# A gated mixer and peer-expert block: 160 of 512 tokens by gathered expert rows instead of 128, the dense units in groups of eight

## The chip, the cores and the metric

The program runs on one core of one Trainium2 chip. The metric is the device time of one execution in microseconds, the median of several. Engines are named as the profile names them: PE is TensorE (PEld its weight loads), DVE is VectorE, ACT is ScalarE, POOL is GpSimd, which issues the indirect DMAs, and SP is the engine whose queue issues the plain ones.

## What is computed

One layer of a model with 512 tokens of width 2048 (a retention branch and an mLSTM branch, merged and projected), then a residual block of "peer" experts and a final norm. The change touches the peer block alone:

```python
def block(tb):                       # tb: 128 tokens x 2048
    qh = (tb @ w_query).reshape(128, 8, 2, 128)
    s = jnp.einsum('thpd,hpkd->thpk', qh, sub_keys)
    sv, si = lax.top_k(s, 16)
    cand_s = sv[:, :, 0, :, None] + sv[:, :, 1, None, :]     # 16 x 16 sums
    cand_i = si[:, :, 0, :, None] * 128 + si[:, :, 1, None, :]
    best_s, best_j = lax.top_k(cand_s.reshape(128, 8, 256), 16)
    eid = jnp.take_along_axis(cand_i.reshape(128, 8, 256), best_j, axis=-1)
    g = jax.nn.softmax(best_s, axis=-1)
    act = gelu(jnp.einsum('thkd,td->thk', expert_down[eid], tb))
    return jnp.einsum('thk,thkd->td', g * act, expert_up[eid])
```

So each token picks 8 heads x 16 = 128 of 16,384 experts; an expert is a row of 2048 in `expert_down` and one in `expert_up`.

## The kernel before

Channels lie on partitions and tokens along the free axis. A float32 matrix product is made of three float32r matmuls: a weight tile `raw` (128 x 1024 from HBM) is split into `ws`, a high half cast on ScalarE and a low half subtracted on VectorE (`weight`), the activations likewise, and `mm3` adds high x high, high x low and low x high. There are seven `raw` and three `ws` buffers. A scheduler lets weight tiles run up to 400 steps ahead of their place in the program.

The peer block (`phase_d`) has three stages. `select` computes the queries (16 tiles of w_query, each 16 blocks of 128 channels by `mm3` on all 512 tokens), scores and picks the experts, mostly on VectorE. `gating` turns the picks of the dense tokens into a table of gates in HBM, by one-hot products. `experts` then evaluates the two kinds of tokens:

- The dense tokens go through all experts as through a wide hidden layer: 128 tiles of 128 hidden units each. A tile's down part is 48 matmuls (`hidden`, PSUM tile `hid`), then gelu on ScalarE (`hf`), the product with the gates (`hf` again, VectorE) and the split into `hh` (ScalarE and VectorE). After a group of GRP tiles their up part runs: 16 output blocks, of which four stay in PSUM all the while (`pac`) and twelve are added to `acc` in SBUF after each group (`upp`). 38 tiles' down parts (NE) run earlier, beside `select` and `gating`, and are parked in HBM.
- The first 128 tokens are *gathered*: one token on each partition, and for each of its 128 picks an indirect DMA on GpSimd brings one row of 2048 for every partition (`row`, 1 MB). For the down table VectorE multiplies it with the tokens (`h2n`) and sums to `dots`; for the up table it adds the row times its weight to `gacc`.

The order of the gathers is written out by hand. `gather(n)` counts units of TensorE's work: 20 for a hidden tile (in two halves) and UP for each of the eight steps of a group's up part (UP0 while the group's tiles were all computed earlier), and calls `row()` whenever the share of rows issued falls behind the share of SPAN. Each call issues a gather and lets VectorE process the one before (LAG = 1). A gather waits for its buffer, one of two (ROW_BUFS), and by `add_manual_dep` for the matmul last issued at its place (`self.last`).

```python
if len(late) > LAG or not slots:
    f, s_, r = late.pop(0)
    f(s_, r)
```

## Time and profile before

| | before |
|---|---|
| median of 3 runs | 4233.39 us |
| lowest, highest | 4217.9, 4237.24 us |
| the profiled execution's own time | 4242.06 us |
| its span, first to last instruction | 4240.3 us |
| PE busy | 4113.0 us (97%) |
| PEld busy | 3668.2 us (87%) |
| DVE busy | 2829.7 us (67%) |
| ACT busy | 1333.7 us (31%) |
| mean granted PE clock (share of full speed) | 0.988 |
| HBM read, written | 851.24, 63.05 MB |

Busy time is the time in which an engine had an instruction in it. Matmuls are pipelined: one starts before the last has ended, so what one costs is read from start to start and not from its length. DVE here means VectorE's own instructions, waits not included. The name before an arrow is the tile that is written, those behind it are read.

### The profile page before, as it was taken

To read this page: it belongs to the slowest core of one execution; us is meant where nothing else is said; L and a number is where in the kernel's file an instruction comes from. 1 tells how busy PE (TensorE), PEld (TensorE's weight loads), DVE (VectorE), ACT (ScalarE), POOL (GpSimd) and SP (SyncE) were. 2 spreads that over 40 slices of the span, in tenths; PEclk is the share of its full clock that TensorE was granted. 3 is DMA by queue.
4 is the path that set the end of the run, shared out by engine and by line. 5 is a ranking of instruction groups with operands and counts; after the bars stand their busy time and mean duration, and the time that the engine had idled before them with its cause. 6 is when DMAs were issued, how large, how long until landed. Compare 5 with 4: busy or idle time off the path is not lost.

```text
span 4240.3 us, 55153 instructions
## 1 busy us (share of the span) xinstructions
PE 4113.0 (97%) x21737; PEld 3668.2 (87%) x21737; DVE 2829.7 (67%) x4504; ACT 1333.7 (31%) x1793; POOL 336.6 (8%) x264
## 2 busy tenths in 40 slices
PE   7999999999999999999999999999999999999998
PEld 3788887777788887898999999999999999999998
DVE  7932238677533433888886766777777777777777
ACT  3322133345322222433443322222323232222223
POOL 0000000000000000000000111111212112111210
PEclk9999999999999999999999999999999999999999
DMA  8522237667633443433456776787878788777784
GB/s 305 203 69 85 70 114 283 218 226 242 223 112 125 150 148 141 147 114 114 166 219 232 257 255 235 287 293 280 297 284 295 285 294 296 285 290 290 293 291 146
DMA packets 288355, 917.90 MB, mean 216 GB/s; under 512 B 26848, under 2 KB 100320, under 8 KB 253664
## 3 DMA queue, kind: packets, MB, share of 16 engines
q1 hardware_dynamic: 248928, 641.74, 43.3%
q0 software_dynamic: 36864, 268.45, 16.7%
q10 hardware_dynamic: 2304, 4.20, 0.3%
q8 instruction: 170, 2.79, 0.3%
q14 instruction: 89, 0.73, 0.1%
HBM read 851.24 MB, written 63.05 MB: 216 GB/s over the span
## 4 chain that ended last, share of the span: by engine, by line
PE 58%; DMA 24%; DVE 9%; issue 8%; ACT 1%; SPq 0%; POOL 0%; DVEq 0%; POOLq 0%; ACTq 0%
DMA row<-in_dnr,eid 11%; PE px L233 9%; PE px L234 9%; PE px L235 9%; DMA row<-in_up,eid 6%; PE hid L233 4%; PE hid L235 4%; PE hid L234 4%; DVE ws L224 3%; DMA gt<-gd 3%; PE va L233 2%; PE va L234 2%; PE va L235 2%; PE upp L235 2%; PE upp L233 2%
## 5 line engine op out<-in xcount | busy, mean ns | idle before, releaser
L223 ACT CAST ws<-raw 128x1024 fp32r<-128x1024 f32 x770 | 809.2, 1051 | 1921.0 <-PE px L235 571.0
L224 DVE TENSOR_TENSOR ws<-raw,ws 128x1024 fp32r<-128x1024 f32 x770 | 939.4, 1221 | 539.2 <-ACT ws L223 534.3
L235 PE MATMUL hid<-h,ws 128*128 128x384 f32 x2048 | 688.1, 336 | 8.7 <-DVE ws L224 8.6
L233 PE MATMUL hid<-h,ws 128*128 128x384 f32 x2048 | 694.9, 339 | 0.2 <-ACT ws L223 0.2
L234 PE MATMUL hid<-h,ws 128*128 128x384 f32 x2048 | 686.2, 335 | 0.0
L233 PE MATMUL upp<-hh,ws 128*128 128x384 f32 x1536 | 520.2, 339 | 19.2 <-DVE acc L1440 16.8
L235 PE MATMUL upp<-hh,ws 128*128 128x384 f32 x1536 | 518.9, 338 | 11.8 <-DVE ws L224 11.8
L234 PE MATMUL upp<-hh,ws 128*128 128x384 f32 x1536 | 517.7, 337 | 0.0
L1263 POOL DMA_INDIRECT row<-in_dnr,eid x128 | 172.0, 1344 | 3071.5 <-DMA gt<-gd 2270.0
L233 PE MATMUL px<-hhi,ws 128*128 128x512 f32 x1024 | 413.1, 403 | 0.0
L1269 DVE SCALAR_TENSOR_TENSOR row<-row,h2n 128x2048 f32<-128x2048 f32 x128 | 293.2, 2291 | 177.0 <-DMA row<-in_dnr,eid 176.9
L234 PE MATMUL px<-hlo,ws 128*128 128x512 f32 x1024 | 407.3, 398 | 0.0
L235 PE MATMUL px<-hhi,ws 128*128 128x512 f32 x1024 | 407.2, 398 | 0.0
L1278 DVE SCALAR_TENSOR_TENSOR gacc<-row,wts,gacc 128x2048 f32<-128x2048 f32 x127 | 298.5, 2350 | 161.0 <-DMA row<-in_up,eid 161.0
L235 PEld LDWEIGHTS hid<-h,ws 128*128 128x128 f32 x2048 | 384.9, 188 | 13.8 <-DVE ws L224 13.4
L233 PEld LDWEIGHTS hid<-h,ws 128*128 128x128 f32 x2048 | 385.3, 188 | 1.1 <-ACT ws L223 0.6
L234 PEld LDWEIGHTS hid<-h,ws 128*128 128x128 f32 x2048 | 385.3, 188 | 0.4
L233 PEld LDWEIGHTS upp<-hh,ws 128*128 128x128 f32 x1536 | 291.3, 190 | 26.9 <-issue 11.3
L235 PEld LDWEIGHTS upp<-hh,ws 128*128 128x128 f32 x1536 | 291.4, 190 | 14.8 <-DVE ws L224 14.7
L234 PEld LDWEIGHTS upp<-hh,ws 128*128 128x128 f32 x1536 | 291.2, 190 | 0.0
L235 PEld LDWEIGHTS px<-hhi,ws 128*128 128x128 f32 x1024 | 192.6, 188 | 47.1 <-issue 2.9
L234 PEld LDWEIGHTS px<-hlo,ws 128*128 128x128 f32 x1024 | 192.7, 188 | 42.2 <-issue 4.6
(426 smaller groups left out, 6198.9 us busy)
## 6 DMA issues: line engine op xcount, KB each, us to landing
raw<-in_dn SPq DMA_DIRECT2D x256, 512.0 KB, 4.1
raw<-in_upt SPq DMA_DIRECT2D x256, 512.0 KB, 4.7
raw<-in_wada_r SPq DMA_DIRECT2D x160, 512.0 KB, 4.6
raw<-in_wt SPq DMA_DIRECT2D x130, 512.0 KB, 3.7
gd<-sg SPq DMA_DIRECT2D x12, 2048.0 KB, 7.5
gt<-gd SPq DMA_DIRECT2D x32, 768.0 KB, 9.5
raw<-in_wada_s SPq DMA_DIRECT2D x32, 512.0 KB, 6.4
raw<-in_wn SPq DMA_DIRECT2D x32, 512.0 KB, 3.6
```

The costliest lines, as they stand in the source:

```text
L223: self.S.copy(w[:, 0], r)
L224: self.V.tensor_sub(w[:, 1], r, w[:, 0].bitcast(F32))
L233: mm(out, lhsT=l[0], rhs=r[0], start=start, stop=False)
L234: mm(out, lhsT=l[0], rhs=r[1], start=False, stop=False)
L235: return mm(out, lhsT=l[1], rhs=r[0], start=False, stop=stop)
L1263: i = G.indirect_dma_start(out=r, out_offset=None, in_=src, in_offset=bass.IndirectOffsetOnAxis(ap=eid[:, s_:s_ + 1], axis=0))
L1269: V.scalar_tensor_tensor(r, r, 1.0, self.h2n, op0=OP.mult, op1=OP.mult, accum_out=dots[:, s_:s_ + 1])
L1278: V.scalar_tensor_tensor(gacc, r, wts[:, s_:s_ + 1], gacc, op0=OP.mult, op1=OP.add)
```

## The change

32 more tokens are gathered. Since there are 128 partitions, each of these tokens stands on four of them (`h2n[1]` holds 32 tokens four times over), and each of the four takes a quarter of the token's 128 picks; so they need 32 gathers in the down table and 32 in the up table, of the same size as the others: 320 in place of 256. The quarters are added at the end by 16 small products with a folded identity (`fold`). Indices and gates of these tokens are brought into that layout by eight small DMAs.

The dense tokens are 352 in place of 384. Because the tokens of a query matmul now lie in two tiles (`h2`, the dense 352, and `h2g`, the gathered 160, which is given back after `select`), each query matmul of 512 columns is written as one of 352 and one of 160. `x1`'s buffers are five in place of eight.

Groups have eight tiles in place of four (GRP), so `acc` is added to half as often; `upt` is laid out in two halves of four tiles a group. UP and UP0 are doubled with it, and SPAN comes to 3644 units for 320 gathers, where it was 3852 for 256.

```diff
-X1_BUFS = 8
+X1_BUFS = 5
-ND = T - P
-GRP = 4
+GX = 32
+G_ = P + GX
+ND = T - G_
+NDB = -(-ND // P)
+GRP = 8
...
-HID, UP, UP0 = 20, 10, 6
+SLOTS = P + GX
+
+
+
+
+HID, UP, UP0 = 20, 10 * GRP // 4, 6 * GRP // 4
...
-        self.h2n = d0.tile([P, D], F32, name="h2n", tag="h2n")
-        self.HF = []
+        self.h2n = [d0.tile([P, D], F32, name=f"h2n{i}", tag=f"h2n{i}") for i in range(2)]
+        self.HG, self.HD = [], []
...
-            h = d0.tile([P, 2, T], F32R, name="h2", bufs=KT)
-            S.activation(h[:, 0], x, AF.Identity, bias=sh2[:, k:k + 1])
-            V.scalar_tensor_tensor(h[:, 1], x, sh2[:, k:k + 1], h[:, 0].bitcast(F32), op0=OP.add, op1=OP.subtract)
-            self.HF.append((h[:, 0], h[:, 1]))
+            h = d0.tile([P, 2, ND], F32R, name="h2", bufs=KT)
+            hg = d1x.tile([P, 2, G_], F32R, name="h2g", bufs=KT)
+            for o, c in ((h, slice(G_, T)), (hg, slice(0, G_))):
+                S.activation(o[:, 0], x[:, c], AF.Identity, bias=sh2[:, k:k + 1])
+                V.scalar_tensor_tensor(o[:, 1], x[:, c], sh2[:, k:k + 1], o[:, 0].bitcast(F32), op0=OP.add, op1=OP.subtract)
+            self.HD.append((h[:, 0], h[:, 1]))
+            self.HG.append((hg[:, 0], hg[:, 1]))
...
+            S.activation(xn[:, k % 4, P:].rearrange("p (q t) -> p q t", t=GX),
+                         x[:, P:G_].unsqueeze(1).to_broadcast([P, P // GX, GX]), AF.Identity, bias=sh2[:, k:k + 1])
...
+            for b, n, o in ((0, P, self.eid[0]), (1, GX, ex)):
+                ef = d1.tile([P, 16], F32, name="ef")
+                V.scalar_tensor_tensor(ef[:n], sel[:n, b, 0, h], float(NKEY), sel[:n, b, 1, h], op0=OP.mult, op1=OP.add)
+                V.tensor_copy(o[:, h], ef[:n])
+            if h == P_H - 1:
+                V.tensor_copy(self.gates[0], sel[:, 0, 2].rearrange("p h k -> p (h k)"))
+                for o, x in ((self.eid[1], ex), (self.gates[1], sel[:GX, 1, 2])):
+                    x = x.rearrange("p h k -> p (h k)")
+                    for q in range(P // GX):
+                        SY.dma_start(o[q * GX:(q + 1) * GX], x[:, q * GX:(q + 1) * GX])
+
+        parts = lambda ps: [(ps[:, G_:], lambda k: self.HD[k]), (ps[:, :G_], lambda k: self.HG[k])]
...
-                    self.tjob([a["wq"][j, 0], a["wq"][j, 1]], [(ps, lambda k: self.HF[k])])
+                    self.tjob([a["wq"][j, 0], a["wq"][j, 1]], parts(ps), one=True)
...
+        def rows(src, i, s_):
             r = d2.tile([P, D], F32, name="row", bufs=ROW_BUFS)
-            i = G.indirect_dma_start(out=r, out_offset=None, in_=src,
-                                     in_offset=bass.IndirectOffsetOnAxis(ap=eid[:, s_:s_ + 1], axis=0))
-            self.tc.add_manual_dep(i.ins, self.last.ins.name, PACE, reason="pace of the gathers")
+            g = G.indirect_dma_start(out=r, out_offset=None, in_=src,
+                                     in_offset=bass.IndirectOffsetOnAxis(ap=eid[i][:, s_:s_ + 1], axis=0))
+            self.tc.add_manual_dep(g.ins, self.last.ins.name, PACE, reason="pace of the gathers")
             return r
...
-        def down(s_, r):
-            V.scalar_tensor_tensor(r, r, 1.0, self.h2n, op0=OP.mult, op1=OP.mult, accum_out=dots[:, s_:s_ + 1])
-            if s_ == P - 1:
-                S.activation(wts, dots, AF.Gelu)
-                V.tensor_mul(wts, wts, gates)
-
-        def up(s_, r):
+        def down(i, s_, r):
+            V.scalar_tensor_tensor(r, r, 1.0, self.h2n[i], op0=OP.mult, op1=OP.mult, accum_out=dots[i][:, s_:s_ + 1])
+            if s_ == dots[i].shape[1] - 1:
+                S.activation(wts[i], dots[i], AF.Gelu)
+                V.tensor_mul(wts[i], wts[i], self.gates[i])
...
-        slots = [(f, w, s_) for f, w in ((down, a["dnr"]), (up, a["up"])) for s_ in range(P)]
+                V.scalar_tensor_tensor(gacc[i], r, wts[i][:, s_:s_ + 1], gacc[i], op0=OP.mult, op1=OP.add)
+
+        slots = [(f, w, i, s_) for f, w in ((down, a["dnr"]), (up, a["up"])) for i, n in enumerate((P, GX)) for s_ in range(n)]
+        NS = len(slots)
...
-            while slots and 256 - len(slots) < 256 * done // SPAN:
+            while slots and NS - len(slots) < NS * done // SPAN:
...
+            ps = self.ps("gtp")
+            for k in range(KT):
+                TE.matmul(ps[:, k * GX:(k + 1) * GX], lhsT=gacc[1][:, k * P:(k + 1) * P], rhs=fold, start=True, stop=True)
...
+            for q in range(GRP // 4):
+                ws = [self.weight(a["upt"][g, u, q]) for u in range(NPA // 2)]
+                for js in (range(3), (3,)) if g == NG - 1 and q == GRP // 4 - 1 else (range(4),):
+                    for d_ in range(NPA):
+                        part(ws[d_ // 2], q, d_, pac[d_], js)
...
+                    ds = (2 * u, 2 * u + 1)
+                    pss = [self.ps("upp") for _ in ds]
+                    for q in range(GRP // 4):
+                        w = self.weight(a["upt"][g, u, q])
+                        for d_, ps in zip(ds, pss):
+                            part(w, q, d_, ps, range(4))
+                            if q < GRP // 4 - 1:
+                                continue
+                            if g == 0:
+                                V.tensor_copy(x2[d_], ps[:, :ND])
+                            elif g < NG - 1:
+                                V.tensor_add(x2[d_], x2[d_], ps[:, :ND])
```

In TensorE's program, in `select`, a query tile's block of 128 channels; `px` is the query's PSUM tile and `h` the normed tokens. Before, two blocks:

```order
L233 MATMUL px<-h_11780,ws 128x512
L234 MATMUL px<-h_11780,ws 128x512
L235 MATMUL px<-h_11780,ws 128x512
L233 MATMUL px<-h_11785,ws 128x512
L234 MATMUL px<-h_11785,ws 128x512
L235 MATMUL px<-h_11785,ws 128x512
```

and now, one block and the start of the next:

```order
L238 MATMUL px<-h_11794,ws 128x352
L239 MATMUL px<-h_11794,ws 128x352
L240 MATMUL px<-h_11794,ws 128x352
L238 MATMUL px<-h2g,ws 128x160
L239 MATMUL px<-h2g,ws 128x160
L240 MATMUL px<-h2g,ws 128x160
L238 MATMUL px<-h_11804,ws 128x352
L239 MATMUL px<-h_11804,ws 128x352
L240 MATMUL px<-h_11804,ws 128x352
```

Three matmuls of 512 have become three of 352 and three of 160.

In VectorE's program, in the middle of `experts`, while hidden tiles are computed; `row` with `dots` is the use of a gathered row. Before:

```order
L1269 SCALAR_TENSOR_TENSOR row,dots<-row,h2n 128x2048
L224 TENSOR_TENSOR ws<-raw,ws 128x1024
L1398 TENSOR_TENSOR hf<-hf,gt 128x384
L1269 SCALAR_TENSOR_TENSOR row,dots<-row,h2n 128x2048
L224 TENSOR_TENSOR ws<-raw,ws 128x1024
L229 TENSOR_TENSOR hh<-hf,hh 128x384
L224 TENSOR_TENSOR ws<-raw,ws 128x1024
L1398 TENSOR_TENSOR hf<-hf,gt 128x384
L229 TENSOR_TENSOR hh<-hf,hh 128x384
L1269 SCALAR_TENSOR_TENSOR row,dots<-row,h2n 128x2048
L224 TENSOR_TENSOR ws<-raw,ws 128x1024
```

and now:

```order
L1445 TENSOR_TENSOR hf<-hf,gt 128x352
L1299 SCALAR_TENSOR_TENSOR row,dots_18626<-row,h2n_11754 128x2048
L234 TENSOR_TENSOR hh<-hf,hh 128x352
L229 TENSOR_TENSOR ws<-raw,ws 128x1024
L1299 SCALAR_TENSOR_TENSOR row,dots_18626<-row,h2n_11754 128x2048
L229 TENSOR_TENSOR ws<-raw,ws 128x1024
L1445 TENSOR_TENSOR hf<-hf,gt 128x352
L1299 SCALAR_TENSOR_TENSOR row,dots_18626<-row,h2n_11754 128x2048
L234 TENSOR_TENSOR hh<-hf,hh 128x352
L229 TENSOR_TENSOR ws<-raw,ws 128x1024
L1299 SCALAR_TENSOR_TENSOR row,dots_18626<-row,h2n_11754 128x2048
L229 TENSOR_TENSOR ws<-raw,ws 128x1024
```

A row stands behind each `ws`; before, two rows stood to three `ws`.

The same engine in the up part of a group, where `acc` takes the sums from `upp`. Before:

```order
L224 TENSOR_TENSOR ws<-raw,ws 128x1024
L1440 TENSOR_TENSOR acc<-acc,upp 128x384 x2
L224 TENSOR_TENSOR ws<-raw,ws 128x1024
L1440 TENSOR_TENSOR acc<-acc,upp 128x384
L1269 SCALAR_TENSOR_TENSOR row,dots<-row,h2n 128x2048
L1440 TENSOR_TENSOR acc<-acc,upp 128x384
L224 TENSOR_TENSOR ws<-raw,ws 128x1024
L1440 TENSOR_TENSOR acc<-acc,upp 128x384 x2
L1269 SCALAR_TENSOR_TENSOR row,dots<-row,h2n 128x2048
L224 TENSOR_TENSOR ws<-raw,ws 128x1024
L1440 TENSOR_TENSOR acc<-acc,upp 128x384 x2
```

and now:

```order
L1494 TENSOR_TENSOR acc<-acc,upp 128x352 x2
L229 TENSOR_TENSOR ws<-raw,ws 128x1024
L1299 SCALAR_TENSOR_TENSOR row,dots_18626<-row,h2n_11754 128x2048
L229 TENSOR_TENSOR ws<-raw,ws 128x1024
L1299 SCALAR_TENSOR_TENSOR row,dots_18626<-row,h2n_11754 128x2048
L1494 TENSOR_TENSOR acc<-acc,upp 128x352 x2
L229 TENSOR_TENSOR ws<-raw,ws 128x1024
L1299 SCALAR_TENSOR_TENSOR row,dots_18626<-row,h2n_11754 128x2048
L229 TENSOR_TENSOR ws<-raw,ws 128x1024
L1299 SCALAR_TENSOR_TENSOR row,dots_18626<-row,h2n_11754 128x2048
L1494 TENSOR_TENSOR acc<-acc,upp 128x352 x2
```

There too each `ws` now has a row behind it: these rows hold six `acc` and four rows, those of before eight `acc` and two.

## Rows read from the trace of the kernel before

**Rows 1.** Stages: length, busy time and instructions by engine, granted clock, DMA share, GB/s.

```profile
core 0: us, PE busy (x) PEld busy (x) DVE busy (x) ACT busy (x) POOL busy (x), PEclk, DMA share, GB/s
1700.00:2048.00 348.00, 345.91 (x1788) 313.23 (x1789) 309.62 (x1006) 136.59 (x179) 0.00 (x0) 0.99 0.35 124
2048.00:2281.00 233.00, 229.99 (x2057) 214.59 (x2056) 199.88 (x285) 100.19 (x151) 0.00 (x0) 0.99 0.57 210
2281.00:2600.00 319.00, 298.84 (x1657) 292.56 (x1655) 219.06 (x292) 92.08 (x109) 36.71 (x26) 0.97 0.70 247
2600.00:4126.00 1526.00, 1475.21 (x8341) 1457.94 (x8341) 1128.85 (x1115) 437.72 (x521) 294.19 (x230) 0.99 0.79 289
4126.00:4240.30 114.30, 97.70 (x560) 96.38 (x558) 82.79 (x152) 36.45 (x53) 1.20 (x1) 0.92 0.45 160
```

**Rows 2.** VectorE's costliest groups, 2600 to 4126 us: busy, mean ns, idle before, releaser.

```profile
L224 DVE TENSOR_TENSOR ws<-raw,ws 128x1024 fp32r<-128x1024 f32 x347 | 422.7, 1220 | 13.1 <-ACT ws L223 13.1
L1278 DVE SCALAR_TENSOR_TENSOR gacc<-row,wts,gacc 128x2048 f32<-128x2048 f32 x125 | 293.8, 2350 | 158.3 <-DMA row<-in_up,eid 158.3
L1269 DVE SCALAR_TENSOR_TENSOR row<-row,h2n 128x2048 f32<-128x2048 f32 x103 | 236.0, 2291 | 149.9 <-DMA row<-in_dnr,eid 149.9
L1440 DVE TENSOR_TENSOR acc<-acc,upp 128x384 f32<-128x384 f32 x264 | 137.0, 550 | 21.6 <-PE upp L235 21.5
L1398 DVE TENSOR_TENSOR hf<-hf,gt 128x384 f32<-128x384 f32 x86 | 47.6, 553 | 34.5 <-DMA gt<-gd 34.5
L229 DVE TENSOR_TENSOR hh<-hf,hh 128x384 fp32r<-128x384 f32 x85 | 47.1, 555 | 16.8 <-ACT hh L228 16.8
```

**Rows 3.** The gathers (GpSimd): duration ns min/median/max, first and last start; landings.

```profile
L1263 POOL DMA_INDIRECT row<-in_dnr,eid x128: 936/1187/3035, 2311.9 to 3282.7; - x128
L1263 POOL DMA_INDIRECT row<-in_up,eid x128: 936/1184/2937, 3295.1 to 4125.9; - x128
...
DMA to landing us min/median/max: 5.3/7.7/12.0
```

**Rows 4.** Timeline of GpSimd, 2744 to 2775 us: start, length, idle time before, releaser.

```profile
2745.97 1.66 POOL L1263 DMA_INDIRECT row<-in_dnr,eid  x1 [2.62 <-DVE acc L1440]
2754.14 1.80 POOL L1263 DMA_INDIRECT row<-in_dnr,eid  x1 [6.52 <-DVE acc L1440]
2758.57 1.65 POOL L1263 DMA_INDIRECT row<-in_dnr,eid  x1 [2.63 <-DVE acc L1440]
2766.18 0.94 POOL L1263 DMA_INDIRECT row<-in_dnr,eid  x1 [5.95 <-PE hid L235]
2770.99 1.19 POOL L1263 DMA_INDIRECT row<-in_dnr,eid  x1 [3.87 <-PE hid L235]
```

**Rows 5.** Timeline of VectorE in the same window, around one row operation.

```profile
2749.63 2.29 DVE L1269 SCALAR_TENSOR_TENSOR row<-row,h2n 128x2048 f32<-128x2048 f32 x1 [1.89 <-DMA row<-in_dnr,eid]
...
2755.52 2.29 DVE L1269 SCALAR_TENSOR_TENSOR row<-row,h2n 128x2048 f32<-128x2048 f32 x1
2757.73 0.09 DVE L1269 DVE_READ_ACCUMULATOR row<-row,h2n 128x1 f32 x1
```

**Rows 6.** Timeline of TensorE: first and last of 56, of 15, of 3 matmuls.

```profile
2999.73 0.34 PE L234 MATMUL hid<-h,ws 128*128 128x384 f32 x1
...
3009.26 0.33 PE L235 MATMUL pac<-hh,ws 128*128 128x384 f32 x1
...
1949.62 0.39 PE L233 MATMUL px<-h,ws 128*128 128x512 f32 x1
...
1952.82 0.39 PE L235 MATMUL px<-h,ws 128*128 128x512 f32 x1
...
460.38 0.28 PE L233 MATMUL pc<-hc,ws 128*128 128x256 f32 x1
...
460.62 0.29 PE L235 MATMUL pc<-hc,ws 128*128 128x256 f32 x1
```

**Rows 7.** Timeline of TensorE's weight loads around narrow matmuls: seven loads, then one.

```profile
1884.08 0.86 PEld L1076 LDWEIGHTS sc<-keys,q 128*128 128x128 f32 x7
1884.86 0.19 PEld L233 LDWEIGHTS px<-h,ws 128*128 128x128 f32 x1
```

More of the change, by code (lines that the diff above doesn't have):

```diff
@@ L241, in flush, with tjob @@
             f()
-    def tjob(self, srcs, targets, nk=KT, order=range(8)):
-        n = 0
+    def tjob(self, srcs, targets, nk=KT, order=range(8), one=False):
+        n, last = 0, len(targets) - 1
         for u, src in enumerate(srcs):
@@ L252, in tjob @@
                 c = slice(k8 * P, (k8 + 1) * P)
-                for ps, rhs in targets:
-                    self.last = self.mm3(ps, (w[:, 0, c], w[:, 1, c]), rhs(u * 8 + k8), n == 0, n == nk - 1)
+                for t, (ps, rhs) in enumerate(targets):
+                    self.last = self.mm3(ps, (w[:, 0, c], w[:, 1, c]), rhs(u * 8 + k8),
+                                         n == 0 and not (one and t), n == nk - 1 and not (one and t < last))
                 n += 1
@@ L281, in rms_rows @@
             for i, x in enumerate(sums):
-                self.TE.matmul(ps[:, b:b + 1], lhsT=x[:, b * P:(b + 1) * P], rhs=self.ones[:, 0:1],
+                x = x[:, b * P:min((b + 1) * P, x.shape[1])]
+                self.TE.matmul(ps[:x.shape[1], b:b + 1], lhsT=x, rhs=self.ones[:, 0:1],
                                start=i == 0, stop=i == len(sums) - 1)
@@ L290, in spread @@
             self.rows(ps, lambda b: r[:, b:b + 1], n)
[L291 removed]
+            self.S.copy(out, ps[:, :out.shape[1]])
         if late is None:
@@ L1071, in select @@
         self.sel = sel
-        self.eid = d0.tile([P, P_H, 16], I32, name="eid")
+        self.eid = [d0.tile([P, P_H, 16], I32, name="eid"), d0.tile([P, GX], I32, name="eidx")]
+        self.gates = [d0.tile([P, n], F32, name=f"gates{n}") for n in (P, GX)]
+        ex = d1.tile([GX, P_H, 16], I32, name="ex", bufs=1)
         def score(j, q, val, idx):
@@ L1125, in select @@
                         for ps, w in zip(pss, ws):
-                            self.mm3(ps, (w[:, 0, c], w[:, 1, c]), self.HF[8 * u + k], u + k == 0, u == 1 and k == 7)
+                            for t, (o, rhs) in enumerate(parts(ps)):
+                                self.mm3(o, (w[:, 0, c], w[:, 1, c]), rhs(8 * u + k), u + k + t == 0, u * t == 1 and k == 7)
             for p in range(2):
@@ L1253, in experts @@
         a, V, S, TE, SY, G, d0 = self.a, self.V, self.S, self.TE, self.SY, self.G, self.d0
-        dots = d0.tile([P, P], F32, name="dots")
-        wts = d0.tile([P, P], F32, name="wts")
-        eid = self.eid.rearrange("p h k -> p (h k)")
-        gates = self.sel[:, 0, 2].rearrange("p h k -> p (h k)")
-        gacc = d0.tile([P, D], F32, name="gacc", tag="h2n")
-        slots = []
-        def rows(src, s_):
+        dots = [d0.tile([P, n], F32, name=f"dots{n}") for n in (P, GX)]
+        wts = [d0.tile([P, n], F32, name=f"wts{n}") for n in (P, GX)]
@@ L1262, in rows @@
+        eid = [self.eid[0].rearrange("p h k -> p (h k)"), self.eid[1]]
+        gacc = [d0.tile([P, D], F32, name=f"gacc{i}", tag=f"h2n{i}") for i in range(2)]
+        fold = d0.tile([P, GX], F32, name="fold")
+        V.tensor_reduce(fold, self.ident.rearrange("p (q t) -> p t q", t=GX), AX.X, OP.add)
+        def rows(src, i, s_):
             r = d2.tile([P, D], F32, name="row", bufs=ROW_BUFS)
-            i = G.indirect_dma_start(out=r, out_offset=None, in_=src,
-                                     in_offset=bass.IndirectOffsetOnAxis(ap=eid[:, s_:s_ + 1], axis=0))
@@ L1412, in experts, with part @@
             hh = hs[GRP * g:GRP * (g + 1)]
-            def part(w, d_, ps, js):
+            def part(w, q, d_, ps, js):
                 own = d_ >= NPA
@@ L1417, in part @@
                     c = slice(j * 256 + d_ % 2 * P, j * 256 + (d_ % 2 + 1) * P)
-                    self.last = self.mm3(ps[:, :ND], (w[:, 0, c], w[:, 1, c]), (hh[j][:, 0], hh[j][:, 1]),
-                                         j == 0 and (own or g == 0), j == GRP - 1 and (own or g == NG - 1))
-            ws = [self.weight(a["upt"][g, u]) for u in range(NPA // 2)]
-            for js in (range(GRP - 1), (GRP - 1,)) if g == NG - 1 else (range(GRP),):
-                for d_ in range(NPA):
-                    part(ws[d_ // 2], d_, pac[d_], js)
+                    i = 4 * q + j
+                    self.last = self.mm3(ps[:, :ND], (w[:, 0, c], w[:, 1, c]), (hh[i][:, 0], hh[i][:, 1]),
+                                         i == 0 and (own or g == 0), i == GRP - 1 and (own or g == NG - 1))
+            for q in range(GRP // 4):
[3 more added lines that the diff above has]
+                        part(ws[d_ // 2], q, d_, pac[d_], js)
             if g == NG - 1:
```

100 lines of the change are left out of this document (52 added, 48 removed).

## Prediction

> **What bounds the kernel now.** I read the stretches first [rows 1]: five rows, one for each stage of the last part of the program. TensorE is busy for 346 of 348 us while tokens are scored, and for 1475 of 1526 us in the long stretch from 2600 to 4126 us in which the experts run and rows are gathered. So TensorE sets the time there, with about 3% of waits; VectorE is busy for 1129 of the 1526 us, and the DMA engines 0.79 at 289 GB/s. Before 1700 us nothing is edited but how far ahead `x1` is fetched.
>
> Second, VectorE's groups in that long stretch [rows 2]. The reader should look at the last column: in front of the operations that use a gathered row VectorE stood idle for 158 + 150 = 308 us, each time until the row landed. Busy and waiting for rows make 1437 of 1526 us. VectorE takes its instructions in order, so what stands behind such a wait (the low halves `ws`, the masked units `hh`) waits as well; TensorE does not notice only because three weight buffers lie in between.
>
> Third, the gathers themselves [rows 3]: 256 of them, a median of 7.7 us from issue to landing, 5.3 at least. They use two buffers in turn, so a gather cannot start until the row two places ahead has been consumed. One view of GpSimd and one of VectorE show this ring at work [rows 4, 5]: the gather at 2745.97 lands and is used from 2755.52 to 2757.82, with the accumulator read; 0.75 us after that, at 2758.57, the next gather into the same buffer starts, and the one after that at 2770.99. Those cycles are 12.6 and 12.4 us for two rows; the other buffer's, 2754.14 to 2766.18, is 12.0. At a median landing the least the ring can do is 0.75 + 7.7 + 2.35 (the longer of the two row operations [rows 2]) = 10.8 us for two rows, **5.4 us a row**. The 230 gathers of the stretch [rows 1] took 1526/230 = 6.63 us each: the ring already ran at 81% of its rate.
>
> **The change part by part.** *Narrower dense matmuls.* From start to start, a float32r matmul takes 0.1733 us at 384 columns (55 steps in 9.53 us), 0.2286 at 512 (14 in 3.20) and 0.120 at 256 [rows 6]. On the line from 256 to 384, 352 columns cost 0.160, a saving of 13.2 ns (on the steeper line from 384 to 512, 13.8). There are 128 x 48 down and 128 x 48 up matmuls: 12,288 x 13.2 ns = 162 us. Of these 38 x 48 = 1824 run ahead of the experts (24 us), 10,464 in them (138 us).
>
> *Narrow query matmuls.* Each of the 768 query matmuls of 512 columns becomes one of 352 and one of 160. No row shows 160 columns. Along the line it would be 0.080; but each has a weight load of its own, and where nothing wide hides it two loads start 0.11 us apart [rows 7], so I take 0.112. A pair then costs 0.272 against 0.228: +44 ns, **+34 us**. Bounds: +9 us on the line; and if a narrow matmul ran like the plain float32 ones (two passes of 0.11 us for 128 columns in [rows 7], so 0.27 for 160), +155 us. I stay with the load, since its row is of the same size (128 x 128, four bytes), and since 256 columns, twice the load, still lie on the line. TensorE is busy throughout this stage, so this is on the path.
>
> The Trainium skill (TensorE: Matmul & The Clock Gate, Back-to-back issue gap) gives about N/2.4 + 2.5 ns, which is 69 ns for 160 columns and would make the pair 149 + 69 = 218 ns against 216, so the split would be free. The trace shows 0.2286 us at 512, and 0.11 between two loads; the rows decide.
>
> *Other work ahead of the experts.* The split, copies and extra transposes of the 32 tokens stand in front of the first query head: per 128 channels one more subtract and two more activations, of some 0.35 us, 16 times on VectorE: I put 6 us. Eight small DMAs for the extra indices and gates stand on SP behind work that is done by then: nothing, and were it not so, a few us of weight loads. One-hot work falls by 32 of 384 tokens, but hidden tiles run beside it: nothing. The experts then start at 2281 + 34 + 6 - 24 = 2297 us.
>
> *First groups.* Groups whose units were computed earlier: now nine of four, then four of eight. TensorE had 1728 matmuls of 0.1733 = 299 us there, and the stretch took 319, so 20 of waits. After: 1536 x 0.160 = 246, plus 20: it ends at 2297 + 266 = 2563 us. By the pacing (320 gathers over SPAN = 3644 units, 4 x 96 = 384 of them here; before 256 over 3852, 432 here) 33 gathers fall in it, 8 us apart, which the ring can do.
>
> *The paced stretch.* The remaining 287 gathers are spread over the other 3260 units of pace, and 20 units are one tile's 48 matmuls, 7.69 us: 1253 us of TensorE, so a gather every 4.4 us. The order shows it: nearly every `ws` on VectorE now has a row behind it, where it was two in three. The ring cannot do 4.4; it can do 5.4 at best. Then VectorE stands at each row until it lands, the next `ws` come late, and TensorE waits for those. More is queued than the ring's own delays: VectorE's work in the stretch is 326 `ws` x 1.22 = 398, 287 rows x 2.33 = 669, 120 `acc` x 0.55 = 66, and about 83 x 1.1 = 91 for `hf` and `hh`, together some 1224 us, 98% of TensorE's 1253 even without any wait. (Without groups of eight the `acc` would have been twice as many.) How close to 5.4 will it come? The three cycles above make 6.15 a row, the mean of the stretch 6.63, and the middle between floor and mean is 6.0. At the head of each second half of a group five rows stand almost together, at one place of TensorE's program, so the ring will also idle now and then. I take **6.1**: 287 x 6.1 = 1751 us, to 4314. Bounds: 5.4 gives 1550, 6.63 gives 1903.
>
> *The end.* The gathers finish one group earlier in units, but groups are twice as long. What follows them is the up part of eight tiles, the down part of seven and the up part of eight, blocks of 48 matmuls each: 23 x 7.69 = 177 us. Before it was 4 + 3 + 4 tiles, 11 x 8.32 = 92, of a stretch of 114 [rows 1], so 22 for the closing; the fold of the 32 tokens adds about 3 on VectorE. 177 + 25 = 202: the end at **4516 us**.
>
> The sum is made against the profiled execution: span 4240.3, time 4242.06, so 1.8 us lie around the span; and its time stands 8.7 above the median of the runs. 4516 + 1.8 - 8.7 = 4509; I say **4505**. In short: 162 us are saved on TensorE, 40 are given to the query stage, and the waits of the paced stretch grow from about 100 us (1526 less the 3420/20 = 171 blocks of 8.32 that its pace stands for) to about 500.
>
> **The rivals.** *The ring keeps up* (faster). Nothing forbids landings from getting shorter, since a slower dense stream leaves the DMA engines freer, and the shortest were 5.3 us [rows 3]. It decides where 287 rows take 4240 - 2563 - 202 = 1475 us, 5.14 a row, which is a landing of 7.2 us with no other delay. At 6.5 us the ring does 4.8 a row: 1378, an end at 4143. If it does not bind at all, the stretch keeps its present ratio to TensorE's work, 1526/1423: 1344, an end at 4109. In that case a group of eight, 123 x 1.07 = 132 us, brings 28 rows, 16 weight tiles and its gates, 44 x 1.05 + 1.4 = 47.6 MB, 361 GB/s, where 289 at a share of 0.79 makes 366 at most: the DMA engines would just be full. Against it: the landings were 7.7 while the DMA engines moved 289 GB/s, and at 6.1 us a row they would move 278, hardly less. Chance 0.12.
>
> The Trainium skill (DMA: Bandwidth & Descriptors, Anatomy of one DMA) would have this rival: it gives 2.0 us plus the bytes at 436 GB/s for a DMA issued by GpSimd, 4.4 us for 1.05 MB, and by it the ring would do 3.75 us a row, would not bind, and the end would be 4109. The trace does not agree: not one of 256 landings took less than 5.3 us.
>
> *The ring and TensorE hinder one another* (slower still). A gather waits for TensorE's position as well, and TensorE, starved by VectorE, reaches it late; in the bunches at the head of each second half the ring then stands. At 6.63 us a row or more the end is from 4668 us. For it: that mean is measured. Against it: there the pace set it, not the ring. The narrow matmuls at their upper bound would give the same, 4516 + 121 = 4637. Chance 0.12 in all.
>
> *VectorE alone is the bound* (some of the gain is lost in it). Rows hide their landings behind other VectorE work, but 1224 us of it plus the present waits that are not for rows (13 + 22 + 35 + 17 [rows 2]) make 1311, and 2563 + 1311 + 202 = 4076, if the rest of TensorE's waits go too: also faster, and counted with the first rival. To end within 0.5% of before, between the cases: 0.03.
>
> **How the numbers follow.** The likeliest case, the ring as the bound between 5.4 and 6.63 us a row, is 4310 to 4660 with a chance of 0.70; a small loss below that 0.03. The range of 8 in 10 reaches into both sides: 4260 to 4690. Half a per cent is about what a measurement of this kernel can tell from no change. Faster 0.12, same 0.03, slower 0.85.
>
> **What would show it.** VectorE's idle time before the row operations should grow from 308 to some 450 us or more in the paced stretch, most gathers should start 0.8 us after a row operation's end rather than behind TensorE, and TensorE's busy share there should fall from 97% to about 72%, with waits for `ws` and `hh` that are now 51 us in all. The first groups should end near 2563, and matmuls of 352 columns follow each other every 0.160 us. I am wrong if landings fall below 7 us, if gathers come 5.1 us apart or closer, or if narrow matmuls cost nearer 0.27 us than 0.11.

## The result and the profile after

The kernel after takes **4418.9 us** (median of 4 runs, 4412.7 to 4435.6) against 4231.2 for the kernel before beside it (4217.9 to 4237.2): ratio 1.044, 95% interval 1.0415 to 1.0465. The profiled execution took 4412.72 us, with a span of 4410.8. All times of this section are of that execution.

The stretches of the kernel after that answer to the last three of [rows 1], with the same columns; the first two are the early groups, and the paced stretch is cut a little ahead of the 34th gather and at the last one (4213.3).

```profile
2300.00:2400.00 100.00, 93.69 (x562) 91.89 (x561) 66.97 (x89) 32.89 (x44) 11.06 (x10) 0.95 0.88 297
2400.00:2575.00 175.00, 165.79 (x1011) 162.94 (x1010) 130.82 (x157) 52.58 (x62) 25.65 (x22) 0.99 0.84 300
2575.00:4213.30 1638.30, 1369.41 (x7894) 1311.65 (x7892) 1165.02 (x1037) 398.67 (x496) 368.12 (x288) 0.96 0.80 299
4213.30:4410.80 197.50, 179.10 (x1117) 177.69 (x1117) 118.22 (x203) 63.46 (x84) 1.16 (x1) 0.95 0.47 152
```

The third row is the one to look at: 1638 us, in which no engine is full. TensorE was busy 97% of the paced stretch before, and 84% now; VectorE 71%, the DMA engines 0.80. Whoever reads shares alone would find no bound here. The idle times before VectorE's groups in that stretch tell it (columns as in [rows 2]):

```profile
L229 DVE TENSOR_TENSOR ws<-raw,ws 128x1024 fp32r<-128x1024 f32 x329 | 400.4, 1221 | 40.9 <-ACT ws L228 40.9
L1308 DVE SCALAR_TENSOR_TENSOR gacc<-row,wts,gacc 128x2048 f32<-128x2048 f32 x156 | 366.8, 2351 | 233.6 <-DMA row<-in_up,eid 191.7 <-DMA row<-in_up,eidx 41.0 <-DVE hf L1445 0.4
L1299 DVE SCALAR_TENSOR_TENSOR row<-row,h2n 128x2048 f32<-128x2048 f32 x129 | 295.6, 2291 | 172.4 <-DMA row<-in_dnr,eid 130.5 <-DMA row<-in_dnr,eidx 41.8
```

VectorE waited 406 us for rows to land, where it was 308. What waits behind it shows in TensorE's waits from 2300 to 4400 us (total, times, longest):

```profile
PE hid L240 <- DVE ws L229: 168.7, 122, 3.9
PE pac L240 <- DVE ws L229: 50.1, 25, 5.5
PE upp L238 <- DVE acc L1494: 29.7, 16, 3.7
```

Who released the gathers on GpSimd in the paced stretch (us, times, longest), first in the kernel before (2600 to 4126 us):

```profile
POOL row L1263 <- PE hid L235: 466.3, 91, 7.8
POOL row L1263 <- PE upp L235: 281.1, 60, 11.0
POOL row L1263 <- PE pac L235: 172.6, 17, 13.6
...
POOL row L1263 <- DVE row L1269: 53.9, 9, 9.0
...
POOL row L1263 <- DVE gacc L1278: 31.1, 6, 8.3
```

and after (2575 to 4213 us):

```profile
POOL row L1293 <- DVE gacc L1308: 406.6, 92, 10.2
POOL row L1293 <- DVE row L1299: 237.9, 60, 7.3
POOL row L1293 <- PE pac L240: 141.3, 11, 21.7
POOL row L1293 <- PE hid L240: 129.4, 35, 6.5
```

Before, a gather was mostly let go by TensorE reaching a place in its program: the pace. By a row operation these rows have 15 of 230 let go before, and 152 of 288 after. They name the wait that came last, which can be another one close by: the gather at 2749.99 in the next rows is put down to `hid`, and starts 0.77 us after a row operation ended. Counted by time, from the 34th gather on, 72 of 223 gathers before and 263 of 287 after start within 1 us of the end of the row operation that frees their buffer. That is the ring of two buffers as the bound. One piece of GpSimd's timeline, to set beside [rows 4, 5]:

```profile
2743.59 1.19 POOL L1293 DMA_INDIRECT row<-in_dnr,eid  x1 [2.16 <-DVE row L1299]
2749.99 1.62 POOL L1293 DMA_INDIRECT row<-in_dnr,eid  x1 [5.21 <-PE hid L240]
2753.77 1.19 POOL L1293 DMA_INDIRECT row<-in_dnr,eid  x1 [2.16 <-DVE row L1299]
2760.23 1.62 POOL L1293 DMA_INDIRECT row<-in_dnr,eid  x1 [5.26 <-DVE hh L234]
2764.18 1.19 POOL L1293 DMA_INDIRECT row<-in_dnr,eid  x1 [2.33 <-DVE row L1299]
```

Each buffer comes round in 10.2 to 10.4 us, two rows, where the three cycles before were 12.0 to 12.6. VectorE uses a row soon after it lands, from the 34th gather on 0.17 us in the mean, where it was 0.52 before. In the same window:

```profile
2746.93 2.29 DVE L1299 SCALAR_TENSOR_TENSOR row<-row,h2n 128x2048 f32<-128x2048 f32 x1 [2.52 <-DMA row<-in_dnr,eid]
...
2750.72 2.29 DVE L1299 SCALAR_TENSOR_TENSOR row<-row,h2n 128x2048 f32<-128x2048 f32 x1
2752.93 0.09 DVE L1299 DVE_READ_ACCUMULATOR row<-row,h2n 128x1 f32 x1
```

The row operation ends at 2753.02 with its read, and the next gather starts at 2753.77, 0.75 us later.

The ring also stands still at times. Another piece of GpSimd's timeline, where rows fall due only behind the product into `pac`:

```profile
2930.80 1.19 POOL L1293 DMA_INDIRECT row<-in_dnr,eid  x1 [4.17 <-DVE row L1299]
2947.66 0.94 POOL L1293 DMA_INDIRECT row<-in_dnr,eid  x1 [15.67 <-PE pac L240]
2948.90 1.64 POOL L1293 DMA_INDIRECT row<-in_dnr,eid  x1 [0.30 <-issue]
```

Counted from the starts of all gathers from the 34th (2581.92) to the last (4213.3): 286 intervals of 5.70 us in the mean. 20 of them are over 8 us, 249 us together; the other 266 take 5.20. I use these three numbers for every kernel below.

None of the three is the ring's own rate. Ten of the 20 intervals (156 us) are stops like the one just shown, with a buffer free for 5 us or more; the other ten end as soon as a row operation frees the buffer. And behind a stop both buffers are free, so that the next gather starts at once (2948.90): these ten short intervals take 16 us together. Without the ten stops and the ten intervals behind them a row takes 5.49 us. The prediction's sum gives the same with means of these rows: (0.75 + 7.75 until the landing + 0.17 until the use + 2.32)/2 = 5.50.

### The profile page after: what moved, and what is told of

It is laid out like the page before. It is cut to its first block, busy times and chain, and to the rows that moved or that the text cites. A ratio compares the mean times of both kernels' runs of the same rounds, so it can differ in the third digit from the quotient of the medians.

```text
span 4410.8 us, 56673 instructions
## 1 busy us (share of the span) xinstructions
PE 4062.8 (92%) x22454; PEld 3612.4 (82%) x22454; DVE 2869.6 (65%) x4445; ACT 1317.5 (30%) x1823; POOL 410.5 (9%) x328
## 4 chain that ended last, share of the span: by engine, by line
PE 52%; DMA 30%; issue 9%; DVE 8%; ACT 1%; SPq 0%; POOL 0%; DVEq 0%; POOLq 0%; ACTq 0%
DMA row<-in_up,eid 10%; DMA row<-in_dnr,eid 10%; PE px L238 9%; PE px L239 9%; PE px L240 9%; DMA row<-in_dnr,eidx 3%; PE hid L238 3%; PE hid L240 3%; PE hid L239 3%; DVE gacc L1308 2%; DMA row<-in_up,eidx 2%; PE va L238 2%; PE va L239 2%; PE va L240 2%; DVE ws L229 2%
## 5 line engine op out<-in xcount | busy, mean ns | idle before, releaser
L228 ACT CAST ws<-raw 128x1024 fp32r<-128x1024 f32 x770 | 799.7, 1048 | 1667.4 <-PE px L240 584.1
L240 PE MATMUL hid<-h,ws 128*128 128x352 f32 x2048 | 683.5, 334 | 169.7 <-DVE ws L229 169.3
L238 PE MATMUL hid<-h,ws 128*128 128x352 f32 x2048 | 683.7, 334 | 2.8 <-DVE acc L1494 1.9
L239 PE MATMUL hid<-h,ws 128*128 128x352 f32 x2048 | 668.5, 326 | 0.0
L240 PEld LDWEIGHTS hid<-h,ws 128*128 128x128 f32 x2048 | 393.5, 192 | 207.7 <-DVE ws L229 207.6
L238 PE MATMUL upp<-hh,ws 128*128 128x352 f32 x1536 | 507.4, 330 | 29.8 <-DVE acc L1494 29.7
L240 PE MATMUL upp<-hh,ws 128*128 128x352 f32 x1536 | 502.6, 327 | 27.8 <-DVE ws L229 27.1
L1308 DVE SCALAR_TENSOR_TENSOR gacc<-row,wts,gacc 128x2048 f32<-128x2048 f32 x158 | 371.5, 2351 | 234.1 <-DMA row<-in_up,eid 191.7
L239 PE MATMUL upp<-hh,ws 128*128 128x352 f32 x1536 | 499.9, 325 | 0.0
L1299 DVE SCALAR_TENSOR_TENSOR row<-row,h2n 128x2048 f32<-128x2048 f32 x160 | 366.5, 2291 | 195.4 <-DMA row<-in_dnr,eid 153.5
L1293 POOL DMA_INDIRECT row<-in_dnr,eid x128 | 160.3, 1253 | 2922.8 <-DMA hf<-hs 2293.2
L239 PEld LDWEIGHTS hid<-h,ws 128*128 128x128 f32 x2048 | 397.7, 194 | 0.0
L238 PEld LDWEIGHTS hid<-h,ws 128*128 128x128 f32 x2048 | 394.1, 192 | 3.6 <-ACT ws L228 3.1
L240 PEld LDWEIGHTS upp<-hh,ws 128*128 128x128 f32 x1536 | 293.7, 191 | 38.3 <-DVE ws L229 38.0
L238 PEld LDWEIGHTS upp<-hh,ws 128*128 128x128 f32 x1536 | 293.6, 191 | 35.0 <-DVE acc L1494 33.0
L239 PEld LDWEIGHTS upp<-hh,ws 128*128 128x128 f32 x1536 | 297.2, 193 | 0.0
L233 ACT CAST hh<-hf 128x352 fp32r<-128x352 f32 x128 | 62.0, 486 | 749.8 <-DVE hf L1445 744.4
```

The costliest lines, as they stand in the source:

```text
L228: self.S.copy(w[:, 0], r)
L233: self.S.copy(hi, src)
L238: mm(out, lhsT=l[0], rhs=r[0], start=start, stop=False)
L239: mm(out, lhsT=l[0], rhs=r[1], start=False, stop=False)
L240: return mm(out, lhsT=l[1], rhs=r[0], start=False, stop=stop)
L1293: g = G.indirect_dma_start(out=r, out_offset=None, in_=src, in_offset=bass.IndirectOffsetOnAxis(ap=eid[i][:, s_:s_ + 1], axis=0))
```

## The experiments

Theory: the two row buffers bound the experts, and what stands between a full ring and the end is lost time (pauses, and the end part without rows). Rivals: VectorE's own work is the bound; the DMA engines are; the query's split costs more than thought. All edits are to the kernel after. Ratios are to the kernel before, run on the same chip; "pauses" are intervals of over 8 us.

| kernel | us | ratio (95%) | mean interval | pauses, their us | other intervals |
|---|---|---|---|---|---|
| after | 4418.9 | 1.044 (1.0415 to 1.0465) | 5.70 | 20, 249 | 5.20 |
| half_rows | 4318.4 | 1.021 (1.0171 to 1.0249) | 5.37 | 16, 246 | 4.78 |
| three_buffers | 4191.8 | 0.9921 (0.9891 to 0.9951) | 4.85 | 28, 346 | 4.03 |
| gates_by_four | 4417.3 | 1.0447 (1.0405 to 1.0489) | 5.69 | 24, 260 | 5.21 |
| no_extra_rows | 4167.4 | 0.9852 (0.9809 to 0.9895) | 6.06 | 24, 293 | 5.32 |
| paced_late | 4320.9 | 1.0202 (1.016 to 1.0245) | 5.89 | 25, 323 | 5.22 |
| groups_of_four | 4339.2 | 1.027 (1.0243 to 1.0297) | 5.59 | 14, 126 | 5.42 |
| wide_narrow_turns | 4417.1 | 1.0444 (1.0405 to 1.0482) | 5.70 | 21, 258 | 5.18 |
| rows_in_product | 4355.6 | 1.0297 (1.0271 to 1.0323) | 5.52 | 9, 84 | 5.40 |
| three_turns_late | 4120.1 | 0.9732 (0.9706 to 0.9757) | 5.26 | 27, 370 | 4.38 |
| three_late_through | 4139.0 | 0.9776 (0.974 to 0.9811) | 5.28 | 27, 271 | 4.79 |
| three_half | 4148.7 | 0.9811 (0.9784 to 0.9839) | 4.76 | 22, 304 | 4.00 |
| three_late | 4126.3 | 0.9742 (0.971 to 0.9773) | 5.23 | 32, 395 | 4.34 |

**A third buffer, and its control.**

```
-ROW_BUFS = 2                        +ROW_BUFS = 3
-LAG = 1                             +LAG = 2
-g, j = divmod(i, GRP)               +g, j = divmod(i, 4)
-gts[g] = d2.tile([P, ND // 32, GRP, 32], ...)   +gts[g] = d2.tile([P, ND // 32, 4, 32], ...)
...
```

The last lines (gates loaded for four tiles at a time) free the room for the buffer; `gates_by_four` has only this part.

> Three row buffers and VectorE two rows behind the issue in place of one; to make room the gates are loaded for four tiles at a time. Ring as the bound: the least a row takes falls from 10.8/2 = 5.4 us to 10.8/3 = 3.6, under the 4.4 at which TensorE asks, so the next bound (VectorE's 1224 us or TensorE's 1253 in the paced stretch, with some waits) gives 4080 to 4200 us. VectorE's or the DMA engines' throughput as the bound: their work is the same, about 4400.

> The control for three buffers: gates loaded for four tiles at a time, still two row buffers. All theories: within 0.5% of the changed kernel, 4400 to 4440 us.

The control moves nothing (4417.3). The third buffer takes 226 us off it and makes the change a gain of 0.8%. Its rows come 4.03 us apart outside the pauses, and VectorE's waits from 2300 to 4400 us are:

```profile
DVE ws L229 <- ACT ws L228: 124.1, 68, 6.5
DVE hf L1445 <- DMA gt<-gd: 120.1, 25, 12.6
DVE row L1299 <- DMA row<-in_dnr,eid: 61.8, 47, 4.3
DVE gacc L1308 <- DMA row<-in_up,eid: 45.9, 43, 4.8
...
DVE row L1299 <- DMA row<-in_dnr,eidx: 14.7, 12, 4.4
DVE gacc L1308 <- DMA row<-in_up,eidx: 8.3, 10, 2.0
```

The rows' waits are now 131 us, where the kernel after had 428 over the same window. VectorE's work and the bytes are the same in both, so neither VectorE alone nor the DMA engines were the bound: from 2600 to 3900 us they moved 350 GB/s, where it was 299.

**Half the row operations.** Each row operation takes 1024 of a row's 2048 columns, so half of the gathered tokens' sums is left out. The gathers are whole.

```
-V.scalar_tensor_tensor(r, r, 1.0, self.h2n[i], ...)
+V.scalar_tensor_tensor(r[:, :D // 2], r[:, :D // 2], 1.0, self.h2n[i][:, :D // 2], ...)
-V.scalar_tensor_tensor(gacc[i], r, wts[i][:, s_:s_ + 1], gacc[i], ...)
+V.scalar_tensor_tensor(gacc[i][:, :D // 2], r[:, :D // 2], wts[i][:, s_:s_ + 1], gacc[i][:, :D // 2], ...)
```

> Leaves out half of VectorE's arithmetic on the gathered rows: each row operation reads 1024 of the row's 2048 columns (dots and gacc then cover half the channels); the gathers still bring the whole rows. Ring of two row buffers as the bound: a cycle of two rows loses one half operation, 1.15 us, so 0.58 us a row x 287 = 165 us less, about 4250 us. VectorE's throughput as the bound: 287 x 1.16 = 333 us less until TensorE binds, about 4100. DMA throughput as the bound: no change, 4419.

Minus 100 us, where the ring theory gave 165: between its figure and no change. VectorE's share of a cycle shrank, and VectorE spent part of what it saved in waiting for rows, 222 + 202 + 50 + 49 = 522 us in its waits from 2300 to 4400 us:

```profile
DVE gacc L1308 <- DMA row<-in_up,eid: 221.8, 91, 5.1
DVE row L1299 <- DMA row<-in_dnr,eid: 201.8, 90, 5.8
...
DVE gacc L1308 <- DMA row<-in_up,eidx: 49.5, 21, 4.1
DVE row L1299 <- DMA row<-in_dnr,eidx: 48.5, 22, 4.5
```

The prediction's formula for the ring, with a row operation of 1.28 us, is (0.75 + 7.7 + 1.28)/2 = 4.87 us a row; without stops and the intervals behind them it took 5.00, 0.49 less than the kernel after (my figure had 0.58). That is 149 us less in these intervals, but the stops grew from 156 to 209 us. They are most of what my figure had left out.

**Without the extra rows.** The 64 gathers of the 32 new tokens and their arithmetic are left out; these tokens' expert sums are zero.

```
-for i, n in enumerate((P, GX)) for s_ in range(n)]
+for i, n in enumerate((P,)) for s_ in range(n)]
+V.memset(gacc[1], 0.0)
```

> Leaves out the 64 gathers of the 32 extra tokens and their arithmetic (these tokens' expert sums are set to zero); everything else of the change stays, the pace is spread over 256 rows. Ring as the bound: 229 rows in the paced stretch x 5.7 = 1305 us in place of 1631, about 4090 us, where the ring and TensorE are about even. VectorE's throughput as the bound: 64 x 2.35 = 150 us less, 4260. DMA throughput as the bound: 67 MB at 300 GB/s, 224 us less, 4195. If the groups of eight or the split query matmuls were the cause: no change.

4167.4: so the 64 rows cost 252 us, and the rest of the change gains 1.5%. That is 77 us above the ring's figure and nearer to that for the DMA engines (4195), which three_buffers has excluded. The figure took 5.70 us for each row; it was 6.06, since here only 173 of 223 gathers from the 34th on start within 1 us of the row operation that frees their buffer. The rest of the change gains less than the narrower matmuls save; that the ring still holds most of the 256 rows fits this, but no run separates it from the longer end part.

**Groups of four again.**

```
-GRP = 8
+GRP = 4
```

> The kernel after with tiles of inner units in groups of four again, as before; the 160 gathered tokens and 352 dense columns stay. Ring theory: the end part without gathers is that of groups of four (114 us before, 197.5 after), so some 80 us of it go to the paced stretch, where the ring has 5.70 us for each row: about 4330 to 4340 us. If groups of eight cost nothing in this change: 4419, no change against the kernel after.

4339.2, as the ring theory said. The stretch behind the last gather, by engine:

```profile
4220.40:4330.70 110.30, 91.29 (x571) 90.05 (x570) 82.58 (x171) 35.11 (x52) 1.16 (x1) 0.92 0.46 159
```

110 us instead of 197.5. So 80 of the 188 us lost go with the groups of eight in this change: they take time from the stretch in which rows can be gathered.

**Rows paced late, and rows inside the product.** The first edit changes the pace's table, the second where it counts.

```
-HID, UP, UP0 = 20, 10 * GRP // 4, 6 * GRP // 4
+HID, UP, UP0 = 20, 10 * GRP // 4, 10 * GRP // 4
-SPAN = ... + NE // GRP * 8 * UP0
+SPAN = ... + NE // GRP * 8 * UP0 + 8 * UP + 4 * HID
```

```
                     for d_ in range(NPA):
                         part(ws[d_ // 2], q, d_, pac[d_], js)
+                        if g < NG - 1 and d_ % 2:
+                            gather((UP if (g + 1) * GRP > NE else UP0) // 2)
...
-                gather(UP if (g + 1) * GRP > NE else UP0)
+                if g == NG - 1 or u >= NPA // 2:
+                    gather(UP if (g + 1) * GRP > NE else UP0)
```

> The kernel after, with the rows' pace alone changed: the first groups of tiles count as longer work in the pace, so that they take about fifty rows and not 33, and the last row is due near the end of the tiles and not 200 us ahead of it. Buffers, tiles and instructions stay. Ring theory (two buffers give a row every 5.70 us, wherever it stands; after the last row 197.5 us of work are left in which no row is gathered): 320 rows from 2334 us at 5.70 us end near 4160, with some 55 to 60 us of products behind them: 4214 to 4225 us, about 195 below the kernel after. If VectorE's or TensorE's own work sets the pace in the experts, spreading changes nothing: 4410 to 4420. If the DMA engines as a whole are the limit, the stretch moves its bytes no faster than the three-buffer kernel did: not below 4190.

> The kernel after, with the pace's steps for the first half of the down product put inside it: rows may now be started in the 15 us of the product into the four standing accumulators, where the kernel after counts those steps only behind it. In the trace of the kernel after 20 of the 286 intervals between rows from row 33 on are over 8 us, 249 us together, most of them at such a product, and the other 266 take 5.20 us in the mean. Theory that the ring loses these pauses for good: with 5.2 to 5.4 us in their place 140 us are gained at most, some 100 if shorter pauses stay: 4280 to 4320 us. If the ring catches up behind each pause (the rows due come at once): 4419, no change.

Both fell short by half. Pacing late gained 98 of 195 us: the last gather stands at 4211.6, not near 4160, and behind it 118 us were left, not 55 to 60. My 5.70 us a row was not the ring's rate but a mean over ring and pauses, and there were more pauses (323 us), likely since more rows fell due per group. Starting rows inside the product gained 63 of the 100 to 140. One of the ten stops is left, and 284 of 287 gathers start within 1 us of the row operation that frees their buffer: 5.52 us a row, the ring by itself. The other intervals went from 5.20 to 5.40 because the short ones behind the stops are gone. My figure had counted all 20 intervals over 8 us as stops; the ten that were cost 156 + 16 - 20 x 5.49 = 62 us, which agrees with the time gained.

**Wide and narrow matmuls in turns.** The query's two targets share one loop over the three products (in outline):

```
-for t, (ps, rhs) in enumerate(targets):
-    self.mm3(ps, (w[:, 0, c], w[:, 1, c]), rhs(k), ...)
+for q, (x, y) in enumerate(((0, 0), (0, 1), (1, 0))):
+    for t, (ps, rhs) in enumerate(targets):
+        mm(ps, lhsT=l[x], rhs=rhs(k)[y], ...)
```

> The kernel after with the query's matmuls in turns: for each of the three products first the 352 columns, then the 160, where the kernel after does the three products of 352 and then the three of 160. Each weight load then has a wide matmul to hide under. Theory that the 160-column matmuls wait for their weight load (0.82 us for three pairs where 0.70 would be their columns): the select is reached 20 to 26 us sooner and the end comes as much sooner, about 4395 us. If the narrow matmuls cost their 0.11 us by themselves: no change, 4419 within 5.

Nothing. TensorE's timeline in the kernel after, three narrow and then three wide:

```profile
1712.91 0.24 PE L238 MATMUL px<-h2g,ws 128*128 128x160 f32 x1
1712.99 0.28 PE L239 MATMUL px<-h2g,ws 128*128 128x160 f32 x1
1713.10 0.28 PE L240 MATMUL px<-h2g,ws 128*128 128x160 f32 x1
1713.21 0.36 PE L238 MATMUL px<-h,ws 128*128 128x352 f32 x1
1713.41 0.32 PE L239 MATMUL px<-h,ws 128*128 128x352 f32 x1
1713.57 0.32 PE L240 MATMUL px<-h,ws 128*128 128x352 f32 x1
1713.73 0.24 PE L238 MATMUL px<-h2g,ws 128*128 128x160 f32 x1
```

and the same stretch in turns:

```profile
1713.00 0.36 PE L246 MATMUL px<-h,ws 128*128 128x352 f32 x1
1713.20 0.24 PE L246 MATMUL px<-h2g,ws 128*128 128x160 f32 x1
1713.28 0.36 PE L246 MATMUL px<-h,ws 128*128 128x352 f32 x1
1713.47 0.24 PE L246 MATMUL px<-h2g,ws 128*128 128x160 f32 x1
1713.54 0.36 PE L246 MATMUL px<-h,ws 128*128 128x352 f32 x1
```

Start to start: 0.08, 0.11, 0.11, 0.20, 0.16, 0.16 = 0.82 us for three pairs; in turns 0.20, 0.08, 0.19 and 0.07, 0.54 for two pairs and 0.82 for three again. In both orders the matmul that comes 0.03 to 0.04 us late is the one two places behind a narrow one. The weight loads fit this. In turns:

```profile
1713.04 0.19 PEld L246 LDWEIGHTS px<-h2g,ws 128*128 128x128 f32 x1
1713.20 0.19 PEld L246 LDWEIGHTS px<-h,ws 128*128 128x128 f32 x1
1713.31 0.19 PEld L246 LDWEIGHTS px<-h2g,ws 128*128 128x128 f32 x1
```

From one load to the next it is 0.16 us by turns with 0.11, and in the kernel after, from 1712.75 on, 0.16, 0.11, 0.12, 0.11, 0.16, 0.16. A load starts no less than 0.11 us behind the last in either order, so each narrow matmul costs 0.11 wherever it stands. That is the second case of the expectation.

The Trainium skill (TensorE: Matmul & The Clock Gate, LDWEIGHTS (loading the stationary operand)) puts a load at columns/1.2 ns, by which an estimate for 128 columns is 107 ns; the loads' starts, 0.11 us apart, agree with it.

**What holds the kernel with three buffers.** Four runs, combinations of the edits above.

> The kernel with three row buffers (4191.75 us), with the query's matmuls in turns and the rows paced late as in the two runs beside it. If TensorE's own work sets the end of the three-buffer kernel: 20 to 26 us from the query and some 20 more from waits for rows that spread out, 4145 to 4165 us. If the experts of the three-buffer kernel are held by their bytes (345 to 370 GB/s in the paced stretch): the query's 20 us are gained, the spreading gains in the end part, where the rate was lower, 4150 to 4175. If neither edit does anything: 4190.

> Three row buffers and rows paced late, with the query's matmuls as in the kernel after and the pace's steps behind the product. If the turns of wide and narrow matmuls do nothing (as when they were tried alone, 4417.1 against 4418.9 us), this takes what the run with the turns took: 4112 to 4128 us, and the steps inside the product cost the three-buffer kernel some 19 us. If the turns are worth 20 us once no ring hides them: 4135 to 4145, as the run with the steps inside the product (4139.0 us).

> Three row buffers, rows paced late, and the pace's steps inside the product; the query's matmuls as in the kernel after. If waits for rows still cost the run with three buffers, late pace and turns (4120.14 us) anything, the 27 pauses of over 8 us in its trace go (370 us in all): 4085 to 4110. If that run is held by TensorE, which is busy 97% of its span, nothing more is to be had: 4115 to 4130, and the turns did nothing there either.

> The kernel with three row buffers (4191.75 us) with VectorE's row operations on 1024 of the 2048 columns, so that it leaves out half of the gathered tokens' sums; the gathers are whole. If bytes hold the three-buffer kernel (345 to 370 GB/s in its paced stretch): no change, 4185 to 4195. If VectorE holds it, through the weight splits and sums that TensorE waits for: some 370 us less work on VectorE, and the 60 to 130 us of TensorE's and VectorE's waits in that stretch come back, 4080 to 4130.

three_turns_late (4120.1) lies below both ranges expected of it, three_late (4126.3) in its first. Pacing late takes another 65 us off the three-buffer kernel, since rows now fill time that was without them: the last gather moves from 3980.8 to 3992.6 of a shorter span. The turns do nothing here either (4120.1 and 4126.3, intervals overlap), and starting rows inside the product gains nothing: 4139.0 us, above both of its ranges and dearer if anything, its interval just overlaps too. Half the row operations give three_buffers 43 us, between what the two theories said: neither bytes nor VectorE holds it alone. The window from 2600 to 3900 us, with the columns of [rows 1], first of after:

```profile
2600.00:3900.00 1300.00, 1087.93 (x6246) 1043.16 (x6246) 920.28 (x842) 316.50 (x393) 292.39 (x227) 0.96 0.80 299
```

of three_half:

```profile
2600.00:3900.00 1300.00, 1227.64 (x7465) 1210.02 (x7465) 823.43 (x982) 377.15 (x465) 313.15 (x273) 0.98 0.93 357
```

and of three_late:

```profile
2600.00:3900.00 1300.00, 1252.67 (x7689) 1240.33 (x7688) 1055.11 (x959) 395.14 (x482) 376.70 (x247) 0.99 0.91 341
```

In three_late TensorE is busy 96% and runs 7689 matmuls where after ran 6246; the clock is back at 0.99; the DMA engines stand at 0.91. There 97 of 287 gathers start within 1 us of the row operation that frees their buffer (199 in three_buffers), the others later. That is TensorE's bound again with the DMA engines close behind: the case that the prediction's first rival had priced at 4109 us. three_late is the version to keep, 2.6% below the kernel before.

## Why the prediction was right, and where it was off

The direction, the cause and the range held; the likeliest time was 86 us too long. Step by step, against the profiled execution:

- *Narrower dense matmuls, 0.160 us each.* Right: the 352-column matmuls follow each other every 0.16 us (rows above). The line of [rows 6] gives a saving of 13.3 ns and not 13.2, 1 us in all.
- *Narrow query matmuls, +34 us, a pair 0.272.* Right: 0.82 us for three pairs, and the select begins at 2079.8 us where it began at 2046.1, 34 later. The upper bound of 0.27 us for a narrow matmul is excluded, and the load as its price fits the loads 0.11 us apart.
- *Other work, +6, experts at 2297.* The first gate tile is issued at 2300.1: 3 us more.
- *First groups to 2563.* The gather that opens the paced stretch starts at 2581.9, so 19 late, 16 of them in the stretch itself; its DMA engines ran at 0.84 to 0.88.
- *The paced stretch, 6.1 us a row.* This is the term that was mis-sized: 5.70 measured. 1631 us lie between the 34th gather and the last, 1751 were predicted, so 120 us too long. The floor of 5.4 was right and a little low: without the stops the ring took 5.49, and 5.52 in rows_in_product. What failed is the step from the floor upwards: I averaged it with 6.15 and 6.63, from three cycles and a stretch of the kernel before, in which the pace and not the ring released most gathers (72 of 223 started within 1 us of the row operation, 263 of 287 after), and a landed row waited 0.52 us in the mean. Once VectorE stands at each row, a row is used 0.17 us after landing, and the ring runs at its floor. What comes on top are stops, as the prediction said of the bunches: ten of them, nine at the product into `pac`, 62 us in all or 0.2 us a row.
- *The end part, 202 us.* 197.5.

The differences are 3 + 16 - 120 - 4.5 = -105.5, and 4516 - 105.5 = 4410.5 against a span of 4410.8.

Of the signs to look for, VectorE's idle time for rows grew, to 406 us and not 450, 263 of 287 gathers follow a row operation within 1 us, and TensorE's waits for `ws` in the paced stretch grew from 20 to 234 us (`ws` and `hh` were 43 there; the prediction's 51 takes in the first groups). TensorE's busy share is 84%, not 72. The prediction divided columns by time, while the profile's busy time holds whole spans of matmuls, 0.32 us where they follow each other at 0.16, so that a part of each wait counts as busy. Besides, some 540 steps took 0.26 to 0.30 us in place of 0.16, 67 us more in all, two thirds of them while the granted clock stood at the lower of its two levels, 1.2 GHz (123 us of the stretch). The Trainium skill (Perfetto Trace Analysis, Identifying the Most-Contended Engine) says that busy time of matmuls is a poor measure of headroom; here 84% busy stood over 1253 us of back-to-back work in 1638, 76%.

The rivals: "the ring keeps up" did not happen with two buffers, since landings stayed at 7.7 us; with three buffers and late pacing it did for two gathers in three. "VectorE alone" is excluded by three_buffers. "The ring and TensorE hinder one another" holds in part: the ten stops cost 62 us, and rows_in_product gained 63 by taking them away.

## What to carry to other kernels

A ring of n buffers has a rate: n over (landing, use, and the 0.75 us between them). Hold it against the rate at which the change will ask, in the stretch where it asks, and count the stretches in which nothing is asked (an end part that grew, a product in which no row falls due) as lost to the ring. When it falls short, look for room for one more buffer before giving up the change: here 2 to 3 turned a loss of 4.4% into a gain of 0.8%, and spreading the requests then made it 2.6%. A mean rate measured while something else set the pace says nothing of the ring's own rate.
